# Layer 0 of a two-layer decoder trunk: head pairs' values in one PSUM bank, the kv latent normed before its split, half of a layernorm on ScalarE, six convolution taps from TensorE to VectorE, and w_out taken by pairs of output blocks

## The chip, the cores and the metric

The kernel runs on one core of a Trainium2 chip. The metric is the device time of one execution in microseconds (us). A core has five engines with instruction queues of their own: TensorE (PE in the profile; its weight loads are PEld), VectorE (DVE), ScalarE (ACT), GpSimd (POOL) and SyncE (SP), which here issues nearly all DMA transfers. Each engine takes its instructions strictly in the order in which they were built; semaphores make one engine wait for another.

## The reference

One sequence of 512 tokens and 1024 channels goes through two layers. Only the mixer of layer 0 is touched by the change:

```python
h = rmsnorm(x, norm_mix_e)
proj = h @ w_in
a, g = proj[..., :512], proj[..., 512:1024]
u = causal_dwconv(a * sigmoid(g), conv_w, conv_b)      # 31 taps per channel
u = silu(layernorm(u, conv_ln_g, conv_ln_b))           # over 512 channels
cq, ckv, kr = split(proj[..., 1024:], (384, 256, 32))
q = (rmsnorm(cq, q_norm_g) @ w_uq)                     # 8 heads, 64 + 32 (rotary)
kv = (rmsnorm(ckv, kv_norm_g) @ w_ukv)                 # 8 heads, 64 key + 64 value
o = causal softmax attention, query blocks of 128
x = x + concat([u, o]) @ w_out
```

After the mixer come a gated MLP with a short convolution (d_ff 2816), in layer 1 a pooling mixer and another such MLP, and a final norm. Everything is float32.

## The kernel before

The activations lie transposed, channels on the 128 partitions and the 512 tokens along the free dimension, so that one block of 128 channels is one tile and its product fills one PSUM bank. Precision is kept by splitting each operand into a high and a low part in a reduced float32 format: `split` and `split_scaled` (lines 96 to 105) let ScalarE round the high part and VectorE subtract it to get the low one, and `mm3` (lines 107 to 110) makes three matmuls of each product: high by high, low by high, high by low. Weights come the same way: `fetch` issues the load on SyncE, `prepare` splits it, `weights()` (line 164) hands out the next one and prepares one ahead; raw, high and low parts have three buffers each.

A builder schedules the program: it takes the operations in the written order as priorities and writes out a fixed order for each engine. It also gives tiles their buffers; a tile of a pool whose buffers are all in use waits until the oldest has been read. PSUM has eight banks: six for tag `ps` (`bank()`), one `aux` and one `conv`.

In layer 0 the work stands in this order.

- Ten projections of the normed input (`project`, line 363): the latents for q (three blocks) and kv (two), the rotary key, and the pairs `a`, `g` of the convolution branch; two of the four pairs come earlier from one joint pass. `latent` splits each latent block as soon as its product is there; the root mean square is applied later: `q_scale` inside the softmax, `r_kv` to the keys by a multiplication with `rows_kv` (line 487) and to the values by the scale of a ScalarE copy (line 582). `spread` turns four columns of norms into rows: VectorE writes four diagonal matrices (line 260), TensorE multiplies them with ones (line 261).
- The depthwise convolution of the four channel blocks (`conv`, line 374). Its taps are background work: `tap` (line 399) is one VectorE operation that adds a scaled and shifted copy of `u` to an accumulator in PSUM; `pump` hands out a few of them behind each step of the main work (`LAT`, `GLU`, `BLK`). In the fourth block the first `PE_TAPS` = 16 of 31 taps are diagonal matmuls on TensorE instead (line 392), with the diagonal written by GpSimd, and the remaining 15 are VectorE's, on the same accumulator in bank `aux`. `close` (line 414) copies an accumulator to a `side` tile.
- Attention, head by head: `scores` makes four score products, which VectorE masks and reduces (line 514) and ScalarE exponentiates and normalises (lines 525 and 532); `transposes` turns the probabilities around on TensorE; `values` multiplies them with the values of a head pair, 128 columns wide, and takes from the bank only the 64 rows of its own head. `split` on these half-height rows gives `att`.
- The output projection: `half` multiplies two blocks of output channels with four input blocks. Its attention part starts while the convolution ends. Then the four `side` tiles are transposed (line 623), VectorE takes mean and variance (lines 625 and 626), `rsqrt` runs a dozen tiny VectorE operations, line 637 normalises, the result is transposed back (line 648) and goes through silu (line 650).
- The convolution part of w_out: for each input block, six output blocks (three weights open at once), then the six residuals, then the last two output blocks.

After that both MLPs follow, which are long rows of `mm3`.

## Time and profile before

| | |
|---|---|
| median of 3 timed runs | 992.45 us (992.34 to 993.73) |
| profiled execution, its time | 993.86 us |
| profiled execution, its span | 992.1 us |
| mean granted TensorE clock | 0.991 |
| busy: TensorE, weight loads | 974.1 us (98%), 799.2 us (81%) |
| busy: VectorE, ScalarE, GpSimd | 588.0 (59%), 402.4 (41%), 69.7 us (7%) |
| matmuls | 4476 |

Times in the trace count from the start of the span. The mixer of layer 0 takes about the first 234 us of it. A row of a timeline gives the start, the duration, the engine, the line of the kernel, the operation, its output and input by name (buffer numbers left out), the shapes and the count; in brackets stands how long the engine had been idle before and what ended that. Durations of neighbouring instructions overlap, since an engine starts the next one while the last one drains; what a further instruction costs in a row is the distance between two starts. The windows give, for a stretch of time, the busy time of each engine and the clock that TensorE was granted, as a share of full speed.

### The profile page before, as it was taken

What the parts mean: (1) busy time and instruction counts of PE and PEld (TensorE: products, weight loads), DVE (VectorE), ACT (ScalarE), POOL (GpSimd) and SP (SyncE); (2) the same over time, 40 slices, a digit from 0 to 9 for tenths busy, and PEclk for the clock granted to TensorE, in tenths of its full rate; (3) what the DMA queues carried; (4) which work ended last, traced back from release to release, by engine and by line L of the source; (5) the groups of instructions that cost most, each with busy time, mean ns of one, the idle gap of its engine ahead of it and who ended that gap; (6) DMA issues with size and microseconds to landing.
All of it is one profiled execution on the core that took longest, in us unless ns stands there. A gap on an engine that the chain in (4) does not pass through costs nothing.

```text
span 992.1 us, 11547 instructions
## 1 busy us (share of the span) xinstructions
PE 974.1 (98%) x4476; PEld 799.2 (81%) x4476; DVE 588.0 (59%) x915; ACT 402.4 (41%) x582; POOL 69.7 (7%) x107
## 2 busy tenths in 40 slices
PE   8999999999999999999999999999999999999996
PEld 6888676777888888888888889888888888888885
DVE  4899989947575656565423338586656565522323
ACT  6435677534343333333222336253334333332321
POOL 5000100004000000000001102200000000000111
PEclk9999999989999999999999999999999999999998
DMA  6323101103233232323223241323232323223212
GB/s 219 127 89 112 39 22 44 64 29 105 100 107 106 85 106 85 106 85 107 91 101 106 85 159 44 107 86 101 90 104 88 106 85 107 93 98 105 86 43 85
DMA packets 29478, 91.99 MB, mean 93 GB/s; under 512 B 4080, under 2 KB 6384, under 8 KB 29424
## 3 DMA queue, kind: packets, MB, share of 16 engines
q1 hardware_dynamic: 28880, 90.74, 27.3%
q8 instruction: 35, 0.57, 0.2%
q10 hardware_dynamic: 544, 0.52, 0.2%
q14 instruction: 19, 0.16, 0.0%
HBM read 89.02 MB, written 2.23 MB: 92 GB/s over the span
## 4 chain that ended last, share of the span: by engine, by line
PE 94%; DVE 3%; DMA 1%; issue 1%; ACT 0%; SPq 0%; DVEq 0%; ACTq 0%
PE ps L108 28%; PE ps L110 28%; PE ps L109 28%; PE ps L511 2%; PE ps L558 2%; PE aux L392 1%; PE ps L546 1%; DVE lo L98 1%; PE aux L261 1%; DMA x<-in_xT_dram 1%; PE aux L239 1%; DVE xgl L103 0%; DMA col<-in_cols_dram 0%; PE ps L870 0%; PE ps L869 0%
## 5 line engine op out<-in xcount | busy, mean ns | idle before, releaser
L108 PE MATMUL ps<-xgh,hi 128*128 128x512 f32 x816 | 319.1, 391 | 2.8 <-ACT hi L97 2.8
L97 ACT CAST hi<-raw 128x1024 fp32r<-128x1024 f32 (+2 forms) x166 | 170.0, 1026 | 371.8 <-PE ps L109 344.3
L110 PE MATMUL ps<-xgh,lo 128*128 128x512 f32 x816 | 318.1, 391 | 1.1 <-DVE lo L98 1.0
L109 PE MATMUL ps<-xgl,hi 128*128 128x512 f32 x816 | 318.2, 390 | 0.0
L98 DVE TENSOR_TENSOR lo<-raw,hi 128x1024 fp32r<-128x1024 f32 (+2 forms) x166 | 201.2, 1214 | 156.8 <-ACT hi L97 156.2
L108 PEld LDWEIGHTS ps<-xgh,hi 128*128 128x128 f32 x816 | 153.6, 188 | 35.3 <-ACT hi L97 3.6
L110 PEld LDWEIGHTS ps<-xgh,lo 128*128 128x128 f32 x816 | 153.4, 188 | 35.0 <-DVE lo L98 3.1
L109 PEld LDWEIGHTS ps<-xgl,hi 128*128 128x128 f32 x816 | 153.6, 188 | 31.6
L108 PE MATMUL ps<-gh,hi 128*128 128x512 f32 (+1 forms) x374 | 141.1, 377 | 0.0
L109 PE MATMUL ps<-gl,hi 128*128 128x512 f32 (+1 forms) x374 | 140.9, 377 | 0.0
L110 PE MATMUL ps<-gh,lo 128*128 128x512 f32 (+1 forms) x374 | 140.8, 376 | 0.0
L110 PEld LDWEIGHTS ps<-gh,lo 128*128 128x128 f32 x374 | 70.4, 188 | 13.0
L108 PEld LDWEIGHTS ps<-gh,hi 128*128 128x128 f32 x374 | 70.4, 188 | 12.9
L109 PEld LDWEIGHTS ps<-gl,hi 128*128 128x128 f32 x374 | 70.4, 188 | 12.8
L698 DVE TENSOR_TENSOR t<-ps,rows 128x512 f32<-128x512 f32 x44 | 30.4, 691 | 77.2 <-PE ps L110 77.2
L226 POOL TENSOR_TENSOR sqr<-sqr,sqr 128x512 f32<-128x512 f32 x33 | 50.3, 1524 | 315.3 <-ACT sqr L224 285.3
L710 DVE TENSOR_TENSOR t<-ps,rows 128x512 f32<-128x512 f32 x44 | 30.4, 690 | 67.3 <-PE ps L110 67.1
L399 DVE SCALAR_TENSOR_TENSOR conv<-u,col,conv 128x512 f32<-128x512 f32 x90 | 67.4, 749 | 2.2 <-ACT conv L382 1.8
L705 DVE SCALAR_TENSOR_TENSOR t<-t,col,t 128x512 f32<-128x512 f32 x88 | 65.6, 748 | 1.4
L708 ACT ACTIVATE t<-t 128x512 f32<-128x512 f32 x44 | 27.8, 631 | 74.7 <-DVE t L705 74.7
L103 DVE SCALAR_TENSOR_TENSOR xgl<-x,col,xgh 128x512 fp32r<-128x512 f32 x32 | 32.7, 1037 | 13.2 <-ACT xgh L102 13.2
L108 PE MATMUL ps<-s,hi 128*128 128x512 f32 x96 | 39.5, 426 | 0.0
(182 smaller groups left out, 818.3 us busy)
## 6 DMA issues: line engine op xcount, KB each, us to landing
raw<-in_w_up_dram SPq DMA_DIRECT2D x88, 512.0 KB, 3.3
raw<-in_w_down_dram SPq DMA_DIRECT2D x44, 512.0 KB, 3.2
raw<-in_w_in_dram SPq DMA_DIRECT2D x10, 512.0 KB, 3.3
raw<-in_w_out_dram SPq DMA_DIRECT2D x8, 512.0 KB, 3.2
x<-in_xT_dram SPq DMA_DIRECT2D x8, 256.0 KB, 5.0
raw<-in_w_in_dram SPq DMA_DIRECT2D x8, 256.0 KB, 3.8
raw<-in_w_uq_dram SPq DMA_DIRECT2D x4, 384.0 KB, 3.1
raw<-in_w_ukv_dram SPq DMA_DIRECT2D x2, 512.0 KB, 4.2
```

The costliest lines, as they stand in the source:

```text
L97: i = act.copy(dst[0], src)
L98: dve.tensor_tensor(dst[1], src, dst[0].bitcast(F32), op=ALU.subtract)
L103: dve.scalar_tensor_tensor(dst[1], src, scale, dst[0].bitcast(F32), op0=ALU.mult, op1=ALU.subtract)
L108: pe.matmul(ps, a[0], b[0], start=start, stop=False)
L109: pe.matmul(ps, a[0], b[1], start=False, stop=False)
L110: pe.matmul(ps, a[1], b[0], start=False, stop=stop)
L226: self.engine.tensor_tensor(self.parts[0], self.parts[0], t, op=ALU.add)
L399: i = dve.scalar_tensor_tensor(st["acc"], u[m][:, j : j + S], c(cw + j), st["acc"], op0=ALU.mult, op1=ALU.add,)
L698: dve.tensor_tensor(ut[:, 2 : 2 + S], pu, rows, op=ALU.mult)
L705: dve.scalar_tensor_tensor(a, ut[:, j : j + S], c(fw + j * NF + f), a, op0=ALU.mult, op1=ALU.add)
L708: act.activation(a, a, AF.Silu)
L710: dve.tensor_tensor(b, pv, rows, op=ALU.mult)
```

## The change

The change has five parts.

1. `PE_TAPS` goes from 16 to 10: six taps of the fourth channel block move from TensorE (with six diagonals on GpSimd) to VectorE.
2. The kv latent is no longer split at once. Its two products stay in PSUM until the norms are known and spread; then VectorE multiplies each with gain and norm, and the normed latent is split. Keys and values need no scaling after that: `keys_of` copies on ScalarE instead of multiplying on VectorE, and the value copies have no scale.
3. A value tile becomes twice as wide: one copy for the even and one for the odd heads, the other head's 64 columns zero (GpSimd clears it, ScalarE copies two strided halves). The two heads of a pair then accumulate in one bank, are computed one after the other, and are split once at full height. The probability tiles `pt` get a third buffer for that.
4. In the layernorm two of the four blocks are copied and normalised on VectorE as before; the other two stay in PSUM and are normalised by ScalarE, with a bias `shift` that is computed for it. The inverse root and this step get a high priority in the schedule.
5. The convolution part of w_out runs by pairs of output blocks, all four input blocks for each, and each pair's residuals follow at once.

```diff
--- before.py
+++ after.py
@@ -37,7 +37,7 @@
 N_COL = C_FB + 2 * NF
 
 WARM = 40
-PE_TAPS = 16
+PE_TAPS = 10
 W_PAD, T_PAD, R_PAD = 48, 16, 120
 GLU, LAT, BLK, END = 3, 4, 2, 0
 
@@ -456,7 +456,12 @@
 
     cq, stat_q = latent(3, C_QG, 384)
     rotary()
-    ckv, stat_kv = latent(2, C_KG, 256)
+
+    kv_ps, ckv, stat_kv = [], [], Squares(256, dve)
+    for m in range(2):
+        kv_ps.append(project())
+        stat_kv.add(kv_ps[m])
+        pump(LAT)
 
     ps = project()
     dve.tensor_tensor(ktab, ktab, rows0, op=ALU.mult)
@@ -465,6 +470,15 @@
     r = rstd([stat_q, stat_kv], floor=floor)
     r_q, r_kv = r[:, 0:4], r[:, 4:8]
     dve.tensor_scalar(q_scale, r_q, SCALE, None, op0=ALU.mult)
+    rows_kv = rows_tile()
+    spread(r_kv, rows_kv)
+    for m in range(2):
+        t = temp()
+        dve.scalar_tensor_tensor(
+            t, kv_ps[m], c(C_KG + m), rows_kv, op0=ALU.mult, op1=ALU.mult
+        )
+        ckv.append(s4())
+        split(pair(ckv[m]), t)
     for _ in range(2):
         ps_a = project()
         pump(GLU)
@@ -479,14 +493,12 @@
         ps = bank()
         for k in range(2):
             mm3(ps, part(wk, k * 4 + hp), pair(ckv[k]), k == 0, k == 1)
-        if hp == 0:
-            spread(r_kv, rows_kv)
         ks = keys[hp % 2]
         for e in range(2):
             a, b = e * 64, e * 64 + 64
-            dve.tensor_tensor(ks[a:b, e, :], ps[a:b, :], rows_kv[a:b, :], op=ALU.mult)
-
-    qs, probs, pts, sums, att = {}, {}, {}, {}, []
+            act.copy(ks[a:b, e, :], ps[a:b, :])
+
+    qs, probs, pts, sums, att, both = {}, {}, {}, {}, [], []
     wq = [None]
 
     def queries(h):
@@ -535,7 +547,7 @@
 
     def transposes(h):
         blocks = probs.pop(h)
-        pt = p_a.tile([P, 1280], F32, tag="pt", bufs=2, name=uid("pt"))
+        pt = p_a.tile([P, 1280], F32, tag="pt", bufs=3, name=uid("pt"))
         at, views = 0, []
         for js in ((0,), (1, 3), (2,)):
             ps = bank()
@@ -550,19 +562,20 @@
         pts[h] = [v for _, v in sorted(views, key=lambda v: v[0])]
 
     def values(h):
+
         hp, e = h // 2, h % 2
         if e == 0:
-            att.append(s4())
-        ps = bank()
+            both.append(bank())
+        ps = both[hp]
         for j, pt in enumerate(pts.pop(h)):
             pe.matmul(
-                ps[:, j * P :], vals[j][:, hp * P : (hp + 1) * P], pt,
-                start=j == 0, stop=j == 3,
+                ps[:, j * P :], vals[j][:, e, hp * P : (hp + 1) * P], pt,
+                start=e == 0 and j == 0, stop=e == 1 and j == 3,
             )
-        a = e * 64
-        split(rows_of(att[hp], a, a + 64), ps[a : a + 64, :])
-
-    rows_kv = rows_tile()
+        if e == 1:
+            att.append(s4())
+            split(pair(att[hp]), ps)
+
     queries(0)
     queries(1)
     ps = bank()
@@ -578,8 +591,14 @@
         ps = bank()
         for k in range(2):
             mm3(ps, pair(ckv[k], j * P, (j + 1) * P), part(wv, k, S), k == 0, k == 1)
-        v = p_a.tile([P, S], F32, tag="v", bufs=4, name=uid("v"))
-        act.activation(v, ps, AF.Copy, scale=r_kv[:, j : j + 1])
+        v = p_a.tile([P, 2, S], F32, tag="v", bufs=4, name=uid("v"))
+        pool.memset(v, 0.0)
+        for e in range(2):
+            mine = (slice(None), slice(None), slice(e * 64, e * 64 + 64))
+            act.copy(
+                v[:, e, :].rearrange("p (a b) -> p a b", b=P)[mine],
+                ps.rearrange("p (a b) -> p a b", b=P)[mine],
+            )
         vals.append(v)
     for h in range(HEADS):
         scores(h)
@@ -589,7 +608,8 @@
             transposes(h - 1)
         if h + 2 < HEADS:
             queries(h + 2)
-        if h >= 2:
+        if h >= 3 and h % 2:
+            values(h - 3)
             values(h - 2)
         pump(END)
     pump(200, 200)
@@ -624,20 +644,32 @@
         st = p_s.tile([P, 6], F32, tag="bn", bufs=2, name=uid("bn"))
         dve.bn_stats(out=st, in_=ps)
         dve.bn_aggr(out=mv[:, i, :], in_=st)
-        yn = temp()
-        act.copy(yn, ps)
-        yts.append(yn)
+        if i < 2:
+            yn = temp()
+            act.copy(yn, ps)
+            ps = yn
+        yts.append(ps)
     values(HEADS - 1)
     half(0, att, (3,), True, w0)
     half(1, att, (3,), True, w1)
     v = small()
     dve.tensor_scalar(v, mv[:, :, 1], EPS, None, op0=ALU.add)
-    r_ln = rsqrt(v)
-    for i in range(4):
-        dve.tensor_scalar(
-            yts[i], yts[i], mv[:, i, 0:1], r_ln[:, i : i + 1],
-            op0=ALU.subtract, op1=ALU.mult,
+    with tc.high_priority():
+        r_ln, shift = rsqrt(v), small()
+        dve.scalar_tensor_tensor(
+            shift, mv[:, :, 0], -1.0, r_ln, op0=ALU.mult, op1=ALU.mult
         )
+        for i in range(2):
+            dve.tensor_scalar(
+                yts[i], yts[i], mv[:, i, 0:1], r_ln[:, i : i + 1],
+                op0=ALU.subtract, op1=ALU.mult,
+            )
+        for i in range(2, 4):
+            yn = temp()
+            act.activation(
+                yn, yts[i], AF.Identity, bias=shift[:, i : i + 1], scale=r_ln[:, i : i + 1]
+            )
+            yts[i] = yn
     us = []
     w2 = weights()
     for m in range(4):
@@ -671,12 +703,10 @@
         if not apart:
             stat.add(x[m])
 
-    ws = [weights(0), weights(0), weights(0)]
-    for k in range(4):
-        for m in range(6):
-            mm3(accs[m], part(ws[m // 2], k * 2 + m % 2), pair(us[k]), False, k == 3)
-    for m in range(6):
-        residual(accs[m], m, C_NF)
+    for mp in range(3):
+        half(mp, us, range(4), False, weights())
+        for m in (2 * mp, 2 * mp + 1):
+            residual(accs[m], m, C_NF)
     half(3, att, range(4), True, weights())
     half(3, us, range(4), False, weights())
     for m in (6, 7):
```

How this moves the instructions shows at three places. The first is on TensorE, where the kv norms are spread into rows (`d` are the diagonals, `aux` the bank). Before, it stood between the first key product and the first value products:

```order
L108 MATMUL ps_943<-s_666,hi_903 128x512
L109 MATMUL ps_943<-s_666,hi_903 128x512
L110 MATMUL ps_943<-s_666,lo_904 128x512
L261 MATMUL aux_950<-d_951,sq 128x128
L261 MATMUL aux_950<-d_954,sq 128x128
L261 MATMUL aux_950<-d_957,sq 128x128
L108 MATMUL ps_972<-hi_939,s_626 128x512
L109 MATMUL ps_972<-lo_940,s_626 128x512
L261 MATMUL aux_950<-d_960,sq 128x128
```

In the new order it stands inside the projection of the third block's gate:

```order
L110 MATMUL ps_762<-xgh_144,lo_673 128x512
L110 MATMUL ps_796<-xgh_137,lo_759 128x512
L261 MATMUL aux_732<-d_733,sq 128x128
L261 MATMUL aux_732<-d_736,sq 128x128
L261 MATMUL aux_732<-d_739,sq 128x128
L108 MATMUL ps_796<-xgh_138,hi_758 128x512
L109 MATMUL ps_796<-xgl_146,hi_758 128x512
L110 MATMUL ps_796<-xgh_138,lo_759 128x512
L261 MATMUL aux_732<-d_742,sq 128x128
```

The spread has moved ahead by two projections and the query products; `xgh` and `xgl` are the input's two parts, of which ten projections are made.

The second place is on VectorE, the last taps and what stands among them (`aux` is the accumulator of the fourth channel block, `conv` that of the third, `lo` a weight split, `s` with `ps` a split of attention output). Before:

```order
L399 SCALAR_TENSOR_TENSOR conv_1274<-u_807,col,conv_1274 128x512
L399 SCALAR_TENSOR_TENSOR aux_1023<-u_885,col,aux_1023 128x512
L98 TENSOR_TENSOR s_1633<-ps_1634,s_1633 64x512
L399 SCALAR_TENSOR_TENSOR aux_1023<-u_885,col,aux_1023 128x512
L98 TENSOR_TENSOR lo_1688<-raw_1685,hi_1687 128x1024
L399 SCALAR_TENSOR_TENSOR aux_1023<-u_885,col,aux_1023 128x512 x8
L98 TENSOR_TENSOR s_1633<-ps_1751,s_1633 64x512
L399 SCALAR_TENSOR_TENSOR aux_1023<-u_885,col,aux_1023 128x512 x2
L98 TENSOR_TENSOR lo_1793<-raw_1790,hi_1792 128x1024
L625 BN_STATS bn_1716<-aux_1711 128x6
```

And now:

```order
L399 SCALAR_TENSOR_TENSOR aux_1035<-u_904,col,aux_1035 128x512
L399 SCALAR_TENSOR_TENSOR conv_1278<-u_826,col,conv_1278 128x512
L98 TENSOR_TENSOR s_1602<-ps_1593,s_1602 128x512
L399 SCALAR_TENSOR_TENSOR aux_1035<-u_904,col,aux_1035 128x512
L98 TENSOR_TENSOR lo_1632<-raw_1629,hi_1631 128x1024
L399 SCALAR_TENSOR_TENSOR aux_1035<-u_904,col,aux_1035 128x512
L98 TENSOR_TENSOR lo_1676<-raw_1673,hi_1675 128x1024
L399 SCALAR_TENSOR_TENSOR aux_1035<-u_904,col,aux_1035 128x512 x11
L98 TENSOR_TENSOR s_1739<-ps_1624,s_1739 128x512
L645 BN_STATS bn_1704<-aux_1699 128x6
```

The run on one accumulator at the end has eleven taps instead of eight and two with a split between, two weight splits stand before it, and the last split of attention output stands behind the last tap.

The third place is on TensorE, around the first transposes of the finished convolution (`side`), here with the waits. Before:

```order
L109 MATMUL ps_1692<-s_1633,hi_1643 128x512
L110 MATMUL ps_1692<-s_1633,lo_1644 128x512
L108 MATMUL ps_1797<-s_1232,hi_1687 128x512 [waits PE_49]
L109 MATMUL ps_1797<-s_1232,hi_1687 128x512
L110 MATMUL ps_1797<-s_1232,lo_1688 128x512
L623 MATMUL aux_1711<-sq,side_427 128x128 [waits Activation_49]
L623 MATMUL aux_1711<-sq,side_436 128x128
L623 MATMUL aux_1711<-sq,side_810 128x128
L623 MATMUL aux_1711<-sq,side_888 128x128
L623 MATMUL conv_1721<-sq,side_888 128x128
L109 MATMUL ps_1796<-s_1404,hi_1687 128x512
```

And now:

```order
L110 MATMUL ps_1784<-s_1325,lo_1676 128x512 [waits DVE_49]
L108 MATMUL ps_1784<-s_1486,hi_1675 128x512
L108 MATMUL ps_1635<-s_1739,hi_1397 128x512 [waits Activation_49]
L108 MATMUL ps_1636<-s_1739,hi_1397 128x512
L643 MATMUL aux_1699<-sq,side_427 128x128 [waits Activation_49]
L643 MATMUL aux_1699<-sq,side_436 128x128
L643 MATMUL aux_1699<-sq,side_829 128x128
L643 MATMUL aux_1699<-sq,side_907 128x128
L643 MATMUL conv_1709<-sq,side_907 128x128
L109 MATMUL ps_1635<-s_1739,hi_1397 128x512 [waits DVE_49]
L110 MATMUL ps_1635<-s_1739,lo_1398 128x512
```

The transposes came after all products of the last attention block (`s_1633`) with the first two weight pairs; now two of these products (`s_1739`) stand before the transposes and ten behind.

## The prediction

> **What bounds the kernel now.** I read the page's busy times first, then the windows by stage, then the timelines of TensorE, VectorE and ScalarE from 60 to 240 us, then groups with shapes kept apart. The page's busy line:
>
> ```profile
> PE 974.1 (98%) x4476; PEld 799.2 (81%) x4476; DVE 588.0 (59%) x915; ACT 402.4 (41%) x582; POOL 69.7 (7%) x107
> ```
>
> TensorE is busy 98% of the span, so a microsecond off its work counts unless another engine then ends later. The windows show where that can happen (columns: length, busy time of the five engines, granted clock, DMA):
>
> ```profile
> core 0: us, PE busy (x) PEld busy (x) DVE busy (x) ACT busy (x) POOL busy (x), PEclk, DMA share, GB/s
> 104.50:172.04 67.54, 67.54 (x283) 45.28 (x282) 63.41 (x157) 50.85 (x122) 7.24 (x12) 1.00 0.09 32
> 172.04:189.41 17.37, 17.37 (x83) 13.56 (x82) 16.20 (x25) 9.05 (x19) 0.00 (x0) 1.00 0.08 30
> 196.40:199.70 3.30, 0.18 (x1) 0.01 (x1) 3.06 (x11) 1.03 (x1) 0.00 (x0) 0.95 0.11 42
> 199.70:206.00 6.30, 5.63 (x21) 4.45 (x22) 2.67 (x6) 4.49 (x8) 0.10 (x1) 0.50 0.23 83
> 206.00:970.00 764.00, 763.16 (x3493) 636.29 (x3492) 403.08 (x511) 276.59 (x347) 43.92 (x69) 1.00 0.28 94
> ```
>
> The first row is attention, from VectorE's first score reduction to its last. TensorE has no idle time in it, but VectorE is busy 63.41 of 67.54 us, and then 16.20 of 17.37 up to the last tap of the depthwise convolution. There is a second engine right behind the first. The next two rows are the layernorm bubble: 3.3 us in which TensorE has almost nothing, then 6.3 us at a granted clock of 0.50. In the 764 us of the last row TensorE idles 0.8 us in all, at a clock of 1.00. In TensorE's timeline (start, duration, line, count) the bubble reads:
>
> ```profile
> 190.88 0.66 PE L623 MATMUL aux<-sq,side 128*128 128x128 f32 x4
> ...
> 196.19 0.39 PE L110 MATMUL ps<-s,lo 128*128 128x512 f32 x1
> 199.72 0.44 PE L648 MATMUL aux<-sq,t 128*128 128x128 f32 x1 [3.14 <-DVE t L637]
> ...
> 203.96 2.06 PE L108 MATMUL ps<-s,hi 128*128 128x512 f32 x4
> ...
> 234.86 0.50 PE L110 MATMUL ps<-xgh,lo 128*128 128x512 f32 x1 [0.84 <-DVE lo L98]
> ```
>
> The transposes at 190.88 wait for the convolution's last group. I call that moment t0. The first product of the convolution branch with w_out stands at 203.96, so 13.1 us after t0. From there on TensorE waits once more, 0.84 us at 234.86 for a weight split. Whatever is won up to 204 us arrives at the end unchanged.
>
> **The change part by part.** The sum is made against the profiled execution (span 992.1 us, time 993.86) and the difference applied to the median of the timed runs, 992.45, which is 1.41 lower.
>
> *Six taps off TensorE.* A tap there is an fp32 matmul recorded in two halves; the chain of waits shows one pair as a piece of 0.86 us:
>
> ```profile
> 104.97 0.86 PE aux L392 x2
> ```
>
> Six pairs at 0.86 are 5.1 us off TensorE. On VectorE a tap has two prices, by what stands before it:
>
> ```profile
> 174.01 0.74 DVE L399 SCALAR_TENSOR_TENSOR aux<-u,col,aux 128x512 f32<-128x512 f32 x1
> 174.67 0.74 DVE L399 SCALAR_TENSOR_TENSOR conv<-u,col,conv 128x512 f32<-128x512 f32 x1
> ...
> 180.10 6.28 DVE L399 SCALAR_TENSOR_TENSOR aux<-u,col,aux 128x512 f32<-128x512 f32 x8
> 187.86 1.55 DVE L399 SCALAR_TENSOR_TENSOR aux<-u,col,aux 128x512 f32<-128x512 f32 x2
> ```
>
> Alternating between two accumulators they start 0.66 us apart; eight into one accumulator take 6.28, which is 0.785 each. By the Trainium skill (VectorE: DVE Perf Modes, "The DRAIN you can't avoid") chained operations cost the same with a semaphore after each as with one at the end; this trace disagrees by 0.125 us per tap, and by that rule at the lower price the run of eleven taps that now ends the convolution would take 7.3 us, not 8.6, and the total would be 1.4 us lower.
>
> *What leaves VectorE in exchange.* These are the groups with shapes kept apart, in attention and the tail:
>
> ```profile
> L98 DVE TENSOR_TENSOR s<-ps,s 64x512 fp32r<-64x512 f32 x8 | 5.5, 686 | 0.9 <-ACT s L97 0.8
> L487 DVE TENSOR_TENSOR keys<-ps,rows 64x512 f32<-64x512 f32 x8 | 5.5, 686 | 0.6 <-PE ps L110 0.5
> L97 ACT CAST s<-ps 64x512 fp32r<-64x512 f32 x8 | 4.6, 578 | 6.9 <-PE ps L558 6.8
> ```
>
> From the first score to the last tap VectorE had 63.41 + 16.20 = 79.6 us of work. Six of the eight key multiplications lie there and go to ScalarE: 6 x 0.69 = -4.1. Eight half-height subtractions become four of full height, which cost the same each (a full-height tap of 512 columns above also takes 0.74), and the last falls behind the last tap: -5 x 0.69 = -3.4. By the order seven more taps stand there (six new, one from before the first score), four at 0.66 and three at 0.785: +5.0. Weight splits stay three. That is 77.1 us, a floor of 104.5 + 77.1 = 181.6 for the last tap, and 182.4 for t0 with ScalarE's copy of the result:
>
> ```profile
> 190.14 0.69 ACT L414 ACTIVATE side<-aux,col 128x512 f32<-128x512 f32 x1
> ```
>
> TensorE's own floor for t0: 190.88 less 5.1, less what the new order puts behind t0, 13 matmuls of w_out (two consecutive ones below start 0.22 us apart; 0.227 over a long run):
>
> ```profile
> 85.80 0.39 PE L110 MATMUL ps<-xgh,lo 128*128 128x512 f32 x1
> 86.02 0.39 PE L108 MATMUL ps<-xgh,hi 128*128 128x512 f32 x1
> ```
>
> 13 x 0.227 = 2.95, so 182.8. The two floors coincide, and then each engine's waits add to the other's. Before, VectorE idled 84.9 - 79.6 = 5.3 us in the same stretch. While taps remain on TensorE (five heads) it leads; in the last three heads and the tail VectorE does. I add 3 us, between 0 and 5.3, and take t0 = 185.7 (182.8 to 188.1): -5.2 us. So the removed 5.1 arrive, but no more: of 7.5 us saved on VectorE the taps take back 5.0.
>
> ScalarE gains six key copies and loses four half-height casts in attention, at 0.58 each: +1.2 us on an engine busy 50.85 of 67.54 us. That is hidden by its idle time; with no cover it would cost 1.2.
>
> *Values as wide tiles.* The zero-padded values give the same matmuls with the same columns, so nothing on TensorE. ScalarE writes them in eight half-size copies. Three of the four memsets on GpSimd wait until the input tiles are free, 24 matmuls after 86.02 or near 91.5 us.
>
> ```profile
> L342 POOL MEMSET ctab<- 64x512 f32 x1 | 0.5, 517 | 0.0
> 100.26 0.69 ACT L582 ACTIVATE v<-ps,s 128x512 f32<-128x512 f32 x1 [0.34 <-PE ps L110]
> ```
>
> At twice that row's columns they take about 1.03 us each (an estimate from it) and end near 94.6, 5.7 us before the first values copy at 100.26. Cost 0; if they took three times as long, about 0.5.
>
> *The kv latent normed first.* The row spread now stands inside the projection of the third block's gate, where TensorE is at about 75.9 us, and it needs VectorE's first diagonal. The two held banks come free after the product with the rotary table.
>
> ```profile
> 75.37 0.62 PE L110 MATMUL ps<-xgh,lo 128*128 128x512 f32 x2
> 71.11 0.16 DVE L248 SCALAR_TENSOR_TENSOR s<-aux,misc 128x4 f32<-128x4 f32 x1 [0.78 <-PE aux L239]
> 76.15 0.28 DVE L260 TENSOR_SCALAR d<-sq,s 128x128 f32<-128x128 f32 x1
> 79.40 0.68 DVE L464 TENSOR_TENSOR t<-ps,ktab 128x512 f32<-128x512 f32 x1
> 72.43 0.60 SPq L347 DMA_DIRECT2D ktab<-rope_rows  x1
> ktab<-rope_rows SPq DMA_DIRECT2D x2, 128.0 KB, 4.1
> ```
>
> Between the statistic at 71.11 and the diagonal at 76.15 stood two weight splits; now one, so the diagonal is there near 75.2. Cost 0; if the split stayed, 0.5 us. The banks: two more VectorE operations of 0.75 behind 79.40 end by 82. The projection that needs one of them starts near 86.6: the last one stood at 86.02 before, and 0.55 of spread comes ahead. The cover is 4 us; without it each late microsecond counts. SyncE's queue now issues a w_uq load, which waits for a weight split, ahead of the four loads of the rotary tables. That puts the last of these near 73.3 instead of 72.43; 4.1 us later it has landed, at 77.4, and VectorE needs it at about 78.7 (78.1 before). Cost 0; if it came late, VectorE would lose up to 1 us, which its lighter first heads absorb.
>
> *Layernorm.* VectorE's path from t0 to the first transpose:
>
> ```profile
> 192.87 1.20 DVE L98 TENSOR_TENSOR lo<-raw,hi 128x1024 fp32r<-128x1024 f32 x1
> 197.49 1.23 DVE L98 TENSOR_TENSOR lo<-raw,hi 128x1024 fp32r<-128x1024 f32 x1
> 199.02 1.92 DVE L637 TENSOR_SCALAR t<-t,misc,s 128x512 f32<-128x512 f32 x4
> ```
>
> Two weight splits lie inside it. In the new order two do again, at other places: ahead of the inverse root instead of inside. The fourth statistic waits for a copy with a cast before it (+0.8), the shift adds 0.2. Four scalings of 0.48 in a row become two beside two on ScalarE (-0.5), and transposes of one bank together release the first activation 0.2 to 0.3 sooner. Sum 0.2, taken as 0, from -1.0 to +1.0.
>
> *The clock.* TensorE ran dry at 196.6 (5.7 after t0) until 199.72, and the windows show 0.50 afterwards. Now 13 more matmuls lie behind t0, so it runs dry at t0 + 8.6 and has transposes again at t0 + 9 to 10. The gap of 3.1 us becomes about 1. At full clock the four products at 203.96 take 0.9 instead of 2.06, and the transposes ahead lose a little: -1.0. By the Trainium skill (TensorE: Matmul & The Clock Gate, "Part 1: The HAM clock gate") the gate halves the clock after an idle window of about 3.4 us, in windows that run freely. The trace agrees in kind: the mean of 0.95 over 196.4 to 199.7 puts the fall near 199.4, some 2.8 us after the last matmul. By that rule the new gap is too short.
>
> *w_out by pairs.* The same 48 products, in another order: the third channel block is needed 14 matmuls (3.2 us) after the first product instead of 36, the fourth 20 (4.5 us) instead of 54. Their splits end like this:
>
> ```profile
> 205.87 1.29 DVE L98 TENSOR_TENSOR s<-t,s 128x512 fp32r<-128x512 f32 x2 [1.08 <-ACT s L97]
> ```
>
> That is 2.6 and 3.2 us after 203.96, so the margin is 0.6 and 1.3 us and the cost 0 (at most 1). The residuals of the first four blocks move ahead, where VectorE is free. The 0.84 us stays: it hangs on a weight buffer.
>
> Sum: -5.2 + 0 - 1.0 = **-6.2 us, so 986.2**.
>
> **Rivals.** (1) *The clock falls anyway*, because between 195 and 199 us TensorE has only sixteen transposes, about half a window. Then -5.2: 987.2. For it: the fall came before 3.4 us of idleness were full. Against: the wait of 0.84 us left the clock at 1.00.
> (2) *VectorE keeps the taps' gain.* If VectorE's idle time up to t0 grows from 5.3 to 7 us instead of shrinking, t0 is at 189.8, and with the clock's gain the sum is -2.1: 990.3. For it: VectorE's 94% before. Against: its work per head falls in the first five heads.
> (3) *Slower: the taps run at the dependent price.* In the new order more taps stand behind a tap on the same accumulator. 73 taps lie in the stretch, and eleven have the high price already. If the other 62 all rose from 0.66 to 0.785 that is +7.7, t0 near 193.4, TensorE blocked at the transposes with 30 ready matmuls queued behind them, and the clock's gain lost to that new gap: +2.5, so 995. Break-even lies at about 42 such taps. Against: between the scores the order still alternates taps with other work.
> (4) *No interlock:* t0 at its floor, 182.8, clock kept: -9, so 983.4.
> That the change does nothing it says is excluded by the order: TensorE has ten taps in it.
>
> **How the numbers follow.** What this kernel's measurement can tell from no change is about 0.2%, 2.0 us. Chances: forecast (-4.5 to -8) 0.55, (1) 0.18, (2) 0.14, (3) 0.06, (4) 0.07. Faster by over 2.0 us: the forecast, (1), (4) and half of (2), 0.87. Same: the other half less 0.01, 0.06. Slower: (3) and that 0.01, 0.07. The range leaves out (3), half of (2) and the far end of (4): 983.6 to 989.9.
>
> **What would show it.** Right: the first full transposes of `side` near 185.7, VectorE's run of eleven taps just before with no idle time, a TensorE gap near 195 of about 1 us with the clock at 1.00, convolution products from 199 on, everything after 240 us earlier by one amount. Wrong: TensorE waiting near 76 or 87 us for the latent; tap pitches of 0.785 in attention; a granted clock of 0.50 after 195; a wait between the pairs of w_out.

## The result, and the profile after

The changed kernel takes 986.75 us (median of 6 runs, 985.52 to 988.44), the kernel before 992.39 (6 runs, 991.56 to 993.73): a ratio of 0.9945, 95% interval 0.9934 to 0.9955. That is 5.64 us less, close to the forecast of 986.2. The profiled execution of the changed kernel has a span of 983.8 us (time 985.52). The page's busy line:

```profile
PE 966.6 (98%) x4464; PEld 795.2 (81%) x4464; DVE 582.5 (59%) x910; ACT 403.4 (41%) x590; POOL 70.4 (7%) x105
```

TensorE still reads 98%, with 7.5 us less work. The two spans differ by 8.3 us, 2.7 more than the medians. Before blaming the change, look at what it does not touch: the opening. Windows of before, then of after:

```profile
16.00:20.00 4.00, 2.94 (x9) 2.03 (x10) 3.51 (x4) 3.36 (x7) 3.92 (x3) 0.81 0.48 149
20.00:24.00 4.00, 4.00 (x15) 3.25 (x14) 2.73 (x4) 1.65 (x4) 4.00 (x5) 0.77 0.41 145
```

```profile
16.00:20.00 4.00, 3.71 (x14) 2.46 (x15) 3.98 (x4) 3.34 (x6) 3.92 (x4) 1.00 0.26 74
20.00:24.00 4.00, 4.00 (x19) 3.29 (x18) 1.95 (x4) 1.31 (x3) 3.92 (x5) 1.00 0.67 220
```

In the profiled execution of before the granted clock fell to 0.81 and 0.77 there, in that of after it did not. The two-column products of line 239 that come next start at 62.38 us before and at 60.35 after: 2.03 us that belong to that execution and not to the change (over the fourteen profiled executions of this study they start between 60.08 and 62.54). The first score product stands at 104.16 us before and 101.71 after, which is another 0.42 us. These are the change's: from the two-column products to the first score it takes 41.75 or 41.78 us in the three executions without part 2 of the change and 41.36 in the eleven with it. In the three, TensorE waits there for a weight split; in before:

```profile
64.53 0.49 PE L110 MATMUL ps<-xgh,lo 128*128 128x512 f32 x1 [0.17 <-DVE lo L98]
```

All that follows is measured from the first score product on, in pieces that end at work which both kernels have: t0 (as in the prediction), the first convolution product with w_out, the first product of the feed-forward block. Windows of before and of after over these pieces:

```profile
104.16:190.88 86.72, 86.68 (x371) 60.02 (x369) 80.68 (x181) 61.48 (x142) 7.24 (x12) 1.00 0.09 31
190.88:203.96 13.08, 9.28 (x47) 7.21 (x47) 9.91 (x28) 6.73 (x11) 0.10 (x1) 0.82 0.37 122
203.96:232.56 28.60, 28.60 (x122) 23.31 (x121) 16.45 (x18) 13.35 (x22) 8.73 (x5) 0.96 0.12 37
```

```profile
101.71:184.65 82.94, 80.48 (x346) 55.38 (x344) 77.09 (x176) 60.73 (x143) 4.33 (x6) 1.00 0.10 32
184.65:198.48 13.83, 12.10 (x60) 9.45 (x60) 9.78 (x28) 7.84 (x11) 0.10 (x1) 0.90 0.35 114
198.48:226.07 27.59, 27.59 (x122) 22.84 (x121) 17.86 (x21) 13.66 (x22) 8.19 (x5) 0.99 0.23 77
226.07:960.00 733.93, 733.93 (x3359) 612.81 (x3358) 384.15 (x493) 265.11 (x330) 35.52 (x64) 1.00 0.28 95
```

The sum of the three, called **the stretch** below, went from 128.40 to 124.36 us: -3.78, +0.75 and -1.01. From the feed-forward block's first product to a landmark near the end (the first two-column product of the last norm, 977.45 before and 969.64 after) it went from 744.89 to 743.57, another -1.32: the last row has no TensorE wait at all, where before one of 0.84 us stood. Together that is -5.36, and -5.78 with the 0.42 us ahead of the first score, beside 5.64 by the medians. The rest of the 8.3 us between the two spans is the opening's 2.03 and 0.51 at the very end, where the four products of the last row spread took 1.19 us before and 0.68 after (1.19 again in taps_back, so not by the change).

TensorE's timeline of after shows where its waits are now:

```profile
162.62 2.18 PE L558 MATMUL ps<-sq,prob 128*128 128x128 f32 x10 [2.12 <-ACT prob L544]
184.65 0.66 PE L643 MATMUL aux<-sq,side 128*128 128x128 f32 x4
192.91 0.39 PE L110 MATMUL ps<-s,lo 128*128 128x512 f32 x1
194.89 1.10 PE L680 MATMUL aux<-sq,t 128*128 128x128 f32 x4 [1.59 <-ACT t L669]
198.48 1.45 PE L108 MATMUL ps<-s,hi 128*128 128x512 f32 x4
```

The wait at 162.62 is new: the transposes of the seventh head wait 2.12 us for probabilities, which wait for VectorE's reductions, and the ten transposes then take 2.18 us instead of 1.25. VectorE's closing run is as priced, 0.788 us per tap, and t0 follows 0.05 us after ScalarE's copy. VectorE's row, and ScalarE's:

```profile
174.74 8.67 DVE L399 SCALAR_TENSOR_TENSOR aux<-u,col,aux 128x512 f32<-128x512 f32 x11
193.63 1.00 DVE L663 TENSOR_SCALAR t<-t,misc,s 128x512 f32<-128x512 f32 x2
```

```profile
183.91 0.69 ACT L414 ACTIVATE side<-aux,col 128x512 f32<-128x512 f32 x1
193.11 1.04 ACT L97 CAST hi<-raw 128x1024 fp32r<-128x1024 f32 x1 [3.96 <-PE ps L109]
194.06 0.77 ACT L669 ACTIVATE t<-aux,s,s 128x512 f32<-128x512 f32 x1
```

In the layernorm the scale was known at 193.63 (VectorE starts then), but ScalarE was still casting a weight and began its half at 194.06. The gap on TensorE is 1.59 us, half of what it was, and yet the clock fell:

```profile
195.00:196.00 1.00, 0.88 (x6) 0.64 (x7) 0.76 (x1) 0.51 (x1) 0.00 (x0) 0.82 0.08 16
196.00:197.00 1.00, 0.98 (x5) 0.58 (x5) 0.00 (x0) 0.89 (x2) 0.00 (x0) 0.50 0.41 57
198.00:199.00 1.00, 1.00 (x5) 0.96 (x5) 0.80 (x2) 1.00 (x3) 0.10 (x1) 0.50 0.49 197
199.00:200.00 1.00, 1.00 (x6) 0.76 (x5) 0.49 (x1) 1.00 (x3) 0.00 (x0) 0.97 0.00 0
```

Half clock lasted from about 195.6 to 199.0, 3.4 us; before it was 6.8, from 199.4 to 206.2. The places that the prediction called covered were covered: the row spread runs without a wait, and GpSimd's clears end at 88.1 us, well before the values copies.

```profile
73.33 0.83 PE L261 MATMUL aux<-d,sq 128*128 128x128 f32 x6
85.39 2.74 POOL L595 MEMSET v<- 128x1024 f32 x3 [59.50 <-PE ps L110]
```

### The profile page after: what moved, and what is told of

Same layout as the page of the kernel before. It is cut to its first block, busy times and chain, and to the rows that moved or that the text cites. A ratio compares the mean times of both kernels' runs of the same rounds, so it can differ in the third digit from the quotient of the medians.

```text
span 983.8 us, 11537 instructions
## 1 busy us (share of the span) xinstructions
PE 966.6 (98%) x4464; PEld 795.2 (81%) x4464; DVE 582.5 (59%) x910; ACT 403.4 (41%) x590; POOL 70.4 (7%) x105
## 4 chain that ended last, share of the span: by engine, by line
PE 95%; DVE 2%; DMA 1%; ACT 1%; SPq 0%; issue 0%; DVEq 0%
PE ps L108 29%; PE ps L109 29%; PE ps L110 29%; PE ps L571 2%; PE ps L523 1%; PE aux L392 1%; PE aux L239 1%; PE ps L558 1%; PE aux L261 1%; DMA col<-in_cols_dram 0%; DMA x<-in_xT_dram 0%; DVE conv L399 0%; PE ps L900 0%; PE ps L899 0%; ACT hi L97 0%
## 5 line engine op out<-in xcount | busy, mean ns | idle before, releaser
L727 POOL MEMSET t<- 128x2 f32 x44 | 4.2, 99 | 491.1 <-DVE t L741 350.3
```

## The experiments

Stretch and t0 are counted from the first score product in the profiled execution; "late part" is the piece from the feed-forward block's first product to the landmark near the end; times are medians, ratios to the kernel before as timed on the same chip (its medians there 992.44, 992.96 and 992.58).

| kernel | taps on TensorE | t0 | stretch | late part | time | ratio, 95% interval |
|---|---|---|---|---|---|---|
| before | 16 | 86.72 | 128.40 | 744.89 | 992.4 | 1 |
| changed | 10 | 82.94 | 124.36 | 743.57 | 986.75 | 0.9945 (0.9934 to 0.9955) |
| taps_alone | 10 | 92.74 | 133.94 | 744.87 | 997.95 | 1.0057 (1.0043 to 1.0071) |
| taps_back | 16 | 80.53 | 121.56 | 743.57 | 984.04 | 0.9917 (0.9905 to 0.9930) |
| ln_back | 10 | 82.93 | 123.53 | 743.58 | 985.73 | 0.9935 (0.9922 to 0.9949) |
| wout_back | 10 | 84.12 | 125.94 | 744.89 | 989.84 | 0.9977 (0.9966 to 0.9988) |
| relief_only | 16 | 80.62 | 121.96 | 744.90 | 985.92 | 0.9934 (0.9920 to 0.9947) |
| alternate | 10 | 80.45 | 123.92 | 743.58 | 986.84 | 0.9939 (0.9927 to 0.9952) |
| taps_13 | 13 | 83.00 | 124.41 | 743.60 | 987.65 | 0.9948 (0.9936 to 0.9961) |
| taps_ln_back | 16 | 80.55 | 121.67 | 743.59 | 984.55 | 0.9919 (0.9905 to 0.9932) |
| wout_alone | 16 | 86.74 | 127.94 | 743.57 | 991.00 | 0.9984 (0.9975 to 0.9993) |
| taps_15 | 15 | 81.42 | 122.23 | 743.58 | 984.75 | 0.9916 (0.9902 to 0.9929) |
| keys_only | 16 | 83.71 | 124.57 | 744.91 | 988.53 | 0.9959 (0.9947 to 0.9972) |
| filler | 10 | 82.92 | 123.65 | 743.60 | 987.21 | 0.9945 (0.9933 to 0.9958) |

The theory at the start was the prediction's: two engines at parity, the taps' 5.1 us arriving because VectorE was relieved. Rivals: TensorE's work alone counts; or the layernorm carries the gain.

### taps_alone

```diff
 (the kernel before)
-PE_TAPS = 16
+PE_TAPS = 10
```

> The kernel before with ten taps on TensorE instead of sixteen, and nothing else of the change. The stretch from the first score product to the first product of the feed-forward block took 128.40 us before and takes 124.36 in the changed kernel; it leaves out the opening, which differed by 2.45 us between the two profiled executions at work that the change does not touch. Two-engine theory: the taps' 5.1 us off TensorE are only there because VectorE was relieved by 7.5 us at the same time. Without the relief six taps put 4.2 to 4.7 us on a VectorE that had 5.3 us of idle time in 86; TensorE then waits for score reductions in the last heads. Stretch 127 to 131, time 991 to 995, convolution end t0 between 86.5 and 90 us after the first score (86.7 before). TensorE theory: VectorE's idle time takes the taps in, stretch 123.3 to 124.4, time 987 to 988.

Measured: 5.5 us slower than before, more than even the two-engine theory said. TensorE's timeline and ScalarE's:

```profile
195.47 1.12 PE L623 MATMUL aux<-sq,side 128*128 128x128 f32 x4 [4.55 <-ACT side L414]
204.10 0.45 PE L648 MATMUL aux<-sq,t 128*128 128x128 f32 x1 [4.14 <-DVE t L637]
```

```profile
194.73 0.69 ACT L414 ACTIVATE side<-aux,col 128x512 f32<-128x512 f32 x1 [2.95 <-DVE aux L399]
```

And its windows from t0 to the first convolution product:

```profile
195.47:200.00 4.53, 3.30 (x13) 2.50 (x13) 2.21 (x5) 1.29 (x3) 0.00 (x0) 0.50 0.12 50
200.00:208.35 8.35, 3.59 (x17) 2.82 (x17) 5.27 (x20) 3.51 (x7) 0.10 (x1) 0.50 0.01 2
```

The last tap ends at 194.7 us, 92.0 after the first score (86.0 before, where the same copy stood at 190.14). TensorE has done everything that it could do without the convolution by 191 us and waits 4.55 us, then 4.14 for the layernorm, and all its work there is at a granted clock of 0.50. Five microseconds of work taken off TensorE became nine of waiting in these two waits alone. The TensorE theory is out.

### taps_back

```diff
 (the changed kernel)
-PE_TAPS = 10
+PE_TAPS = 16
```

> The changed kernel with all sixteen taps on TensorE again, the rest of the change kept. Two-engine theory: TensorE has 5.1 us more work and VectorE 4.4 us less, so the wait of 2.1 us at the transposes of the seventh head (with its slow transposes worth about 3.0) is gone: stretch 124.36 + 5.1 - 3.0 = 126.5, time 988.9 (988 to 990). TensorE theory: the full 5.1 us come back, stretch 129.5, time 991.9. Layernorm theory (the gain comes from the layernorm part and not from the taps): stretch 124 to 125, time 986.5 to 987.5.

Measured: 984.04 us, faster than the changed kernel, outside everything expected. The intervals of the two ratios just part (0.9930 and 0.9934), and the stretch is 2.80 us shorter. Its windows:

```profile
101.75:182.28 80.53, 80.41 (x343) 55.35 (x342) 73.09 (x169) 60.66 (x142) 7.96 (x12) 1.00 0.10 33
182.28:195.99 13.71, 13.71 (x77) 11.02 (x75) 10.32 (x28) 8.49 (x12) 0.10 (x1) 1.00 0.20 62
195.99:223.31 27.32, 27.32 (x123) 22.61 (x122) 18.08 (x20) 13.68 (x22) 8.19 (x5) 1.00 0.31 105
```

TensorE has 0.12 us idle in the first piece and none after it, and the clock is 1.00 throughout. Beside it the row of after, 12.10 busy of 13.83, shows what ten taps do: TensorE runs out of work in the layernorm. With sixteen, 77 matmul records lie between t0 and the first convolution product (60 in after, 47 before): attention's products with w_out, which now cover the layernorm. Taking the six taps off TensorE is not a gain in this kernel; it costs 2.7 us. So the two-engine theory falls in its main point, and a new one is needed: **VectorE's work up to t0 decides, and TensorE's taps are free cover.** ScalarE's copy in this run shows already where that ends:

```profile
180.42 0.69 ACT L414 ACTIVATE side<-aux,col 128x512 f32<-128x512 f32 x1 [1.87 <-DVE aux L399]
```

The copy is done at 181.11, but t0 is 182.28. With sixteen taps and the relief VectorE is 1.2 us ahead, and TensorE, busy for 121.44 of the stretch's 121.56 us, comes last. From there on a tap on TensorE need not be free any more.

### ln_back

```diff
 (the changed kernel)
-        if i < 2:
-            yn = temp(); act.copy(yn, ps); ps = yn
-        yts.append(ps)
+        yn = temp(); act.copy(yn, ps); yts.append(yn)
...
+    r_ln = rsqrt(v)                     # no high priority, no shift
+    for i in range(4): dve.tensor_scalar(yts[i], ...)   # all four on VectorE
```

> The changed kernel with the layernorm as before: four copies on ScalarE, four scalings on VectorE, no priority. Two-engine theory: the path from t0 to the first product of the convolution branch was 13.08 us before and is 13.83 in the changed kernel, so this part saves nothing by itself: 13.1 to 13.9, stretch 123.6 to 125.0, time 986.0 to 987.4. Layernorm theory: the shorter gap and the half-clock piece of 3.4 us instead of 6.3 us come from this part; they lengthen again, stretch 126 to 127.5, time 988.5 to 990.

Measured: stretch 0.83 us shorter than in the changed kernel, 13.26 us from t0 to the convolution's product instead of 13.83, and time 985.73. The layernorm theory is out: this part saves nothing, and if anything costs 0.6 us of path (the cast ahead of ScalarE's half accounts for 0.43 of the wait; in this execution the granted clock also stayed at 1.00). The two times alone do not tell the kernels apart.

### wout_back

```diff
 (the changed kernel)
-    for mp in range(3):
-        half(mp, us, range(4), False, weights())
-        for m in (2 * mp, 2 * mp + 1): residual(accs[m], m, C_NF)
+    ws = [weights(0), weights(0), weights(0)]
+    for k in range(4):
+        for m in range(6): mm3(accs[m], part(ws[m // 2], ...), pair(us[k]), ...)
+    for m in range(6): residual(accs[m], m, C_NF)
```

> The changed kernel with the convolution branch's w_out products in the order before (three weight tiles held, channel block outside). Pair theory: after 200 us TensorE no longer waits in the changed kernel, where before it waited 0.84 us for a weight split in the first feed-forward projection; pairs give weight buffers back earlier, and here the wait returns: 0.5 to 1.0 us of TensorE wait for a low half at the feed-forward block's first tile, time 987.3 to 988.0. Chance theory: the wait depended on when transfers of that one execution came, no wait here either, time within 0.4 of 986.75. In both the stretch up to the feed-forward block stays 124 to 125.

Measured: the wait of 0.84 us is back and the late part is 744.89 again, so the pair theory holds where it spoke. But the time rose by 3.1, and the stretch by 1.58. The windows of this run after the wait at the seventh head:

```profile
163.00:165.00 2.00, 1.49 (x6) 0.95 (x7) 2.00 (x5) 2.00 (x5) 0.00 (x0) 0.73 0.00 0
165.00:167.00 2.00, 2.00 (x8) 1.48 (x7) 2.00 (x6) 2.00 (x7) 0.00 (x0) 0.50 0.04 8
167.00:169.00 2.00, 2.00 (x8) 1.25 (x8) 2.00 (x5) 1.79 (x6) 0.00 (x0) 0.92 0.00 0
```

The same wait of 2.1 us that passed at full clock in the changed kernel's profile is followed here by half clock. Nothing of w_out has run by then, so this is not the order of w_out; why all seven timed runs are nonetheless above 989.3 stays open.

### relief_only

The new theory's test: only parts 2 and 3 of the change (latent normed first, key copies on ScalarE, values by pairs), everything else as before. 
```diff
 (the kernel before)
-    ckv, stat_kv = latent(2, C_KG, 256)
+    kv_ps, ckv, stat_kv = [], [], Squares(256, dve)      # normed after its products
...
-            dve.tensor_tensor(ks[a:b, e, :], ps[a:b, :], rows_kv[a:b, :], op=ALU.mult)
+            act.copy(ks[a:b, e, :], ps[a:b, :])
...
+        if e == 1:                                       # both heads in one bank
+            att.append(s4())
+            split(pair(att[hp]), ps)
```

> The kernel before with only the relief of VectorE: the kv latent normed ahead of its split, key copies on ScalarE, values of a head pair in one bank. Sixteen taps on TensorE, layernorm and w_out order as before. VectorE theory (new, after the taps were put back and the time fell): the moment t0 is set by VectorE's work alone, so this part carries the gain. t0 about 80.5 us after the first score (80.53 with the taps put back, 86.72 before), then the layernorm path of 13.1 to 13.8, the 1.3 us of the late w_out weights still lost: stretch 121.5 to 122.5, time 985.5 to 987. TensorE theory (98% busy, its own work is what counts): relieving VectorE without taking work off TensorE gives nothing, stretch 127.5 to 128.5, time 991.5 to 992.5.

Measured: 985.92 us, stretch 121.96, t0 80.62, the numbers of the VectorE theory. Its windows:

```profile
101.86:182.48 80.62, 80.50 (x344) 55.36 (x343) 73.08 (x169) 60.64 (x142) 7.95 (x12) 1.00 0.10 33
182.48:196.29 13.81, 13.81 (x76) 11.00 (x75) 11.01 (x29) 8.14 (x12) 0.10 (x1) 1.00 0.17 50
```

VectorE's busy time up to t0 is 73.08 us instead of 80.68, and TensorE, without one operation less, is busy through the whole layernorm. Here too ScalarE's copy is done (181.23) 1.25 us before t0, so VectorE was late before and is not any more. These two parts alone make 6.6 us (ratio 0.9934). That is at least about as much as the whole change (0.9945): the intervals of the two ratios overlap, but the stretch is 2.40 us shorter.

### alternate

```diff
 (the changed kernel, in conv)
...
+        if m == 3:     # last taps of group 2 and group 3 in turns
+            n = len(work) - len(mine)
+            theirs, work[n:] = work[n:], []
+            for a, b in zip(theirs, mine): work.extend((a, b))
...
```

> The changed kernel (ten taps on TensorE) with the last taps of the third and fourth group issued in turns, so that no run of taps into one accumulator ends the convolution. VectorE theory: the eleven-tap run of 8.67 us becomes 22 alternating taps at 0.66; 11 x 0.125 = 1.4 us off VectorE ahead of t0, t0 81.5 us after the first score (82.94 in the changed kernel), stretch 123.0, time 985.3. TensorE theory: t0 is not bound by the taps' pitch, stretch 124.4, time 986.8. A third outcome: the fourth group's taps start earlier, all ten TensorE taps are issued ahead of them in one piece and delay a score block: t0 unchanged or up to 0.9 later.

Measured: t0 came 2.5 us earlier, and the time did not move. VectorE's timeline, and TensorE's:

```profile
180.70 0.75 DVE L399 SCALAR_TENSOR_TENSOR conv<-u,col,conv 128x512 f32<-128x512 f32 x1
181.35 0.75 DVE L399 SCALAR_TENSOR_TENSOR aux<-u,col,aux 128x512 f32<-128x512 f32 x1
182.01 2.35 DVE L98 TENSOR_TENSOR lo<-raw,hi 128x1024 fp32r<-128x1024 f32 x2
184.28 0.69 DVE L651 BATCH_NORM_STATS2 bn<-aux 128x6 f32<-128x512 f32 x1
```

```profile
164.39 1.46 PE L564 MATMUL ps<-sq,prob 128*128 128x128 f32 x6 [2.79 <-ACT prob L550]
```

The taps do start 0.66 us apart in turns, so their price is what the prediction said. But two weight splits, held back so far, then stand ahead of the layernorm's statistics, the path from t0 grows from 13.83 to 16.11, and the wait at the seventh head to 2.8. The VectorE theory was right that t0 comes earlier (it said 1.4 us; the two splits moved behind t0 add to that) and too simple on the time: work that VectorE owes moves behind t0.

### taps_13 and taps_15

```diff
 (the changed kernel)
-PE_TAPS = 10
+PE_TAPS = 13      (taps_15: 15)
```

> The changed kernel with thirteen taps on TensorE. With sixteen the stretch was 121.56 us, every microsecond of it TensorE work, with ten 124.36 and 4.2 us of waits. VectorE theory: three taps are half of the way, and VectorE sets t0 in both: stretch 122.9, time 985.4. Balance theory: with sixteen TensorE is the bound and with ten VectorE, so the least lies between: TensorE has 2.6 us less, VectorE 2 us more; stretch 119.5 to 121.3, time 982 to 983.7.

> The changed kernel with fifteen taps on TensorE. At sixteen TensorE paced both ends: VectorE had finished the convolution 1.2 us before its transposes came up, and the layernorm's rows were ready 0.3 us before theirs. Parity theory: one more tap costs VectorE 0.79 in the closing run, inside the 1.2; TensorE loses 0.86; the layernorm then ends last: gain 0.3 to 0.6, stretch 121.0 to 121.3, time 983.4 to 983.9. Sharp-edge theory (thirteen taps were as bad as ten): a tap in the closing run moves t0 and with it everything, stretch 122.0 to 122.4, time 984.5 to 985.

Measured: thirteen are no better than ten (t0 83.00, stretch 124.41), fifteen a little worse than sixteen in the profile (81.42, 122.23) and the same in time. The closing runs of taps_13 and of taps_15 on VectorE:

```profile
171.78 11.04 DVE L399 SCALAR_TENSOR_TENSOR aux<-u,col,aux 128x512 f32<-128x512 f32 x14
```

```profile
173.81 9.45 DVE L399 SCALAR_TENSOR_TENSOR aux<-u,col,aux 128x512 f32<-128x512 f32 x12
```

Eleven taps at sixteen became twelve and fourteen: each tap that TensorE gives up from sixteen on lands in the closing run, at 0.79 us. From thirteen to ten the run is eleven again, since TensorE's taps, two per head, are through after five heads instead of seven, and VectorE's can lie between the scores of the last three. There TensorE pays in another way: its last tap starts 37.6 us after the first score (61.8 in taps_back), so it is at the seventh head's transposes early and waits 2.12 us, although VectorE is through with that head's reductions at 60.2 us, earlier than the 61.8 of taps_back. Balance and parity theories are out, the sharp edge holds. In both runs ScalarE's copy ends 1.3 us before t0, as it does by 1.2 in the runs with sixteen taps and the relief, so t0 follows there from TensorE's written order and not from a wait for VectorE. Why that order puts t0 later with fifteen taps than with sixteen is not shown, and an order that puts those transposes ahead of some products was not tried.

### taps_ln_back

```diff
 (ln_back)
-PE_TAPS = 10
+PE_TAPS = 16
```

> The changed kernel with sixteen taps on TensorE and the layernorm as before. With the layernorm part undone at ten taps the stretch went from 124.36 to 123.53 us. Cover theory: at sixteen taps TensorE has no wait in the layernorm (13.71 us busy of 13.71 from t0 to the first product of the convolution branch), so the layernorm's path is covered and undoing its change moves nothing: stretch 121.2 to 121.9, time 983.6 to 984.5. Layernorm theory: its new path costs 0.8 us wherever it stands: stretch 120.7, time 983.2.

Measured: stretch 121.67, time 984.55: no difference from taps_back. Where TensorE has products left, the layernorm's path is covered, whichever way it is written.

### wout_alone

```diff
 (the kernel before)
-    ws = [weights(0), weights(0), weights(0)]
-    for k in range(4):
-        for m in range(6): mm3(accs[m], part(ws[m // 2], ...), pair(us[k]), ...)
-    for m in range(6): residual(accs[m], m, C_NF)
+    for mp in range(3):
+        half(mp, us, range(4), False, weights())
+        for m in (2 * mp, 2 * mp + 1): residual(accs[m], m, C_NF)
```

> The kernel before with only w_out by pairs. Late-weights theory: from the first product of the feed-forward block to the near-last matmuls the orders with three held weight tiles took 744.88 us (before, and with this part undone) and the paired ones 743.57, so pairs are worth 1.3 us there, the wait of 0.84 us among it; stretch unchanged, 128 to 128.6, time 991.1 to 991.9 by a before of 992.5. Face-value theory: undoing this part in the changed kernel cost 3.1 us, so it is worth that here too: time 989.2 to 990.0. In the first, the other 1.8 us of that run were a piece of half clock after the wait at the seventh head, which this part does not touch.

Measured: 991.00, ratio 0.9984, and a late part of 743.57 as in every kernel with pairs. So pairs are worth 1.3 us by the profile and 1.6 by the time; the 3.1 of wout_back was not theirs alone.

### keys_only

```diff
 (relief_only; values of each head in a bank of their own again)
-        if e == 1:
-            att.append(s4())
-            split(pair(att[hp]), ps)
+        a = e * 64
+        split(rows_of(att[hp], a, a + 64), ps[a : a + 64, :])
```

> The kernel before with half of the relief: the kv latent normed ahead of its split and key copies on ScalarE; the values of each head in their own bank with half-height splits as before. Sixteen taps, layernorm and w_out as before. VectorE theory: of 7.5 us of relief 4.1 are here. With both halves VectorE ended 1.2 us before TensorE; without the values' 3.4 it ends 2.2 after it: t0 82.5 to 83.5 us after the first score, stretch 123.5 to 125, time 988 to 989.5. TensorE theory: the order of TensorE's products in the last heads is what counts, and the pair order of the values does that: stretch 127 or more, time over 991.

Measured: 988.53, t0 83.71, stretch 124.57: as the VectorE theory said. ScalarE's timeline shows a detail:

```profile
185.10 0.58 ACT L97 CAST s<-ps 64x512 fp32r<-64x512 f32 x1 [5.89 <-PE ps L570]
185.71 0.69 ACT L414 ACTIVATE side<-aux,col 128x512 f32<-128x512 f32 x1
```

VectorE's last tap ended at 184.3, but the copy of the result stood on ScalarE behind a cast that waited for TensorE's values. That is 1.4 us of the 3.1 us by which t0 is later than in relief_only; fewer and later splits are thus part of what the pairs of heads bring.

### filler

```diff
 (the changed kernel, ahead of the layernorm's transposes)
+        if m == 0:
+            for _ in range(20):
+                pe.matmul(accs[5][:, :P], idle, idle, start=False, stop=False)
```

> The changed kernel (ten taps) with twenty bf16 products of zeros, added to an accumulator between the last product ahead of the layernorm's transposes and these; they add nothing to any value. Clock theory: the wait of 1.59 us at the layernorm is filled, the granted clock stays at 1.00 from 193 to 200 us (it fell to 0.50 for 3.4 us in the profiled execution), the path from t0 to the first product of the convolution branch shortens from 13.83 to 13.2, stretch 123.6, time 986.1. Chance theory: the clock's fall depends on where a gap meets it (it did not fall after a gap of the same size with thirteen taps), fillers or not: time 986.4 to 987.2.

Measured: stretch 123.65, as the clock theory said, but the time of 987.21 cannot be told from the changed kernel's. The fillers did not stand where I meant them: they ran four microseconds earlier, ahead of the products.

```profile
191.66 1.29 PE L681 MATMUL ps<-idle 128*128 128x128 bf16 x20
195.81 0.55 PE L684 MATMUL aux<-sq,t 128*128 128x128 f32 x3 [0.24 <-ACT t L670]
198.09 0.66 PE L684 MATMUL aux<-sq,t 128*128 128x128 f32 x4 [0.85 <-ACT t L686]
```

Products took the gap, 0.24 and 0.85 us of waits remained, and the clock stayed at 1.00 from 186 to 202 us. That makes 0.7 us in one execution. Over the runs it makes nothing that can be seen. The new order also puts the weight cast behind ScalarE's half of the layernorm instead of ahead of it (the half starts at 194.97, right when the scale is known), so this run changes more than the clock, and what the clock alone costs stays open.

## Why the prediction was right, and where it was not

The time came out at 986.75 where 986.2 was forecast. **The sum was right and its largest term stood for the wrong part of the change.** That the sum held is in part luck. From the profiles, t0 came 3.78 us earlier where 5.2 was forecast, and the layernorm's piece took 0.75 more where 0 was. Gains that the prediction put at 0 made most of that good: 1.32 us behind the feed-forward block's first product and 0.42 ahead of the first score. Putting the parts together one after the other (ratios above, times 992.4): relief of VectorE -6.6, pairs of w_out -1.5, layernorm -0.2 (none that can be told), six taps +2.8; that is -5.5.

*Six taps off TensorE: wrong.* The step reads "So the removed 5.1 arrive, but no more: of 7.5 us saved on VectorE the taps take back 5.0." The runs showed the reverse: with all sixteen taps on TensorE t0 comes at 80.53 us after the first score, not later than in the changed kernel but 2.4 us earlier. The error lies in "TensorE is busy 98% of the span, so a microsecond off its work counts". In the stretch of before TensorE was busy while it waited: it did attention's w_out products ahead of t0 and had few left for the layernorm. The stretch held 128.40 - 121.56 = 6.84 us of waits and half clock, 3.8 of it as waits in the timeline, and nearly all of that could be won without taking any work off TensorE, by an earlier t0 that leaves products to cover the layernorm. The prediction had 13 more products behind t0, in its floor and in its clock term. It did not ask how many there would be with the taps left on TensorE: by the windows' records it is 30 more than before (77 to 47), enough to close the gap. Its two floors for t0 were 182.4 and 182.8 us, 78.2 and 78.6 after the first score; measured was 82.94.

*The interlock of 3 us:* its own size was 4.3 (82.94 less 78.6), inside the 0 to 5.3 given. About 3 us of it are one wait of 2.12 us on TensorE at the seventh head and the slow transposes behind it, and not many small waits.

*VectorE's work:* right. Busy time up to t0 fell from 80.68 to 77.09 us, 3.6 where 2.5 was worked out; the tap prices of 0.66 and 0.785 held (0.66 in turns, 0.788 in closing runs of 11, 12 and 14). The Trainium skill (VectorE: DVE Perf Modes, "The DRAIN you can't avoid") reports that eight copies took as long with a semaphore after each as with one after the last. No run here repeats that with copies; taps that read what the tap just before them wrote cost 0.13 us more each than taps in turns, so the prediction was right not to price them by that rule.

*Layernorm, 0:* +0.75 from t0 to the product, inside the ±1.0. The cast that sat ahead of ScalarE's half was not in the sum.

*The clock, -1.0:* the fall came all the same, as rival (1) had it, but shorter. The piece from the first convolution product to the feed-forward block became 1.01 us shorter; about 0.2 of that is the order by pairs (27.53 us in relief_only, 27.35 in taps_ln_back, both at a clock of 1.00). The number nearly held, the reason ("the new gap is too short") did not. The Trainium skill (TensorE: Matmul & The Clock Gate, "Part 1: The HAM clock gate") asks for an idle window of about 3.4 us; here the gap was 1.59 us and the fall still came, lasting 3.4 us.

*w_out by pairs, 0, and "the 0.84 us stays":* wrong by 1.3 us. The wait is there in all five profiled executions with the order before and in none of the nine with pairs. It hung on a weight buffer, as the prediction says; that pairs hand weight buffers back earlier is read from the code.

*Covers of the kv latent, banks, rotary table, clears:* right, no wait at any of them, and the kv latent's new order won the 0.42 us ahead of the first score instead of 0.

*Rivals.* (2) is not what happened, VectorE's idle time up to t0 stayed (6.04, then 5.85 us). (3) named taps as the danger, and taps without the relief do lose 5.5 us, but by their number and not by a change of price. No rival asked what the change would be worth without its taps; that would have been the useful one: 984.

The best version found is the change without its first part (taps_back): 984.04 us, 0.9917 (0.9905 to 0.9930) of the kernel before.

## What to carry to other kernels

An engine that reads 98% busy need not be the bound where it spends its reserve of independent work while it waits: between two fixed points, count how much of that reserve is left behind the latest dependency, and what it covers. Work moved off that engine onto the one that sets the dependency can then be lost twice, as lateness there and as missing cover here. When a change has several parts that share one gain, time the change without each of them before giving the gain to the part with the largest price.

## What the runs showed of the hardware

- The granted clock fell to 0.50 after TensorE waits of 1.59 us (the layernorm, in the changed kernel and in wout_back) and 2.12 us (wout_back's seventh head), each time for 3.4 us by the windows, and after 3.14 us in the kernel before, for 6.8. It did not fall after 2.12 us in the changed kernel's attention, nor after 2.79 us in alternate's, nor after 0.94 and 0.76 us in ln_back. Between the openings of two executions such a piece went with a difference of 2.0 us.
- Taps into one accumulator started 0.788 us apart, in turns 0.66; in alternate the order in turns brought t0 forward by 2.5 us, and the time did not change.
- Twenty bf16 products of 128 columns took 1.1 us, 0.055 each.
